# A hybrid decoder layer on one core: earlier fetches of kept results, finished rows on GpSimd's queue, and loads tied to products

## The chip, the cores and the metric

The kernel runs on one core of one Trainium2 chip. The metric is device time in microseconds (us), from the start to the end of one execution. A result is the median of several executions. The engines are named as in the profile: PE is TensorE's matmul pipe and PEld its weight loads, DVE is VectorE, ACT is ScalarE, POOL is GpSimd, SP is the engine that only issues DMAs here. A DMA that an engine issues goes through that engine's queue.

## The reference

One decoder layer over 2048 tokens of width 1024, in float32. Constants: 8 query heads and 2 key-value heads of 64, a window of 128, a causal convolution of 31 taps over 512 channels, and an inner width of 2816.

```python
hn = rms_norm(h, mix_pre_g)
proj = hn @ w_in                       # q, k, v and the input of the convolution
attn_out = sliding_window_attention(q, k, v, attn_sinks, rel_bias)
conv_out = conformer_conv(u, ...)      # GLU, 31 taps, layer norm, silu, pointwise product
mixed = concatenate([attn_out, conv_out]) @ w_out
h = h + rms_norm(mixed, mix_post_g)
hn = rms_norm(h, ffn_pre_g)
ff = (silu(hn @ w_gate) * (hn @ w_up)) @ w_down
h = h + rms_norm(ff, ffn_post_g)
```

## The kernel before, in words

**Products.** Each float32 operand is split into a high and a low part in fp32r (`split_w`, `split_f`, `lo`): ACT copies the high part, DVE or POOL subtracts it to get the low part. A product then takes three matmuls of 128x512 per block of 128 in the contraction, all of them recorded at line L85. Nearly all DVE operations are recorded at one line too, L94, so they are told apart by the names of their tiles. A letter behind the @ is the stage: A input projection, B attention, C convolution, W output projection, H operands of the channel mixer, F gate and up products, G down products.

**Stages.** The 2048 tokens are four tiles of 512 (0 to 3). A0 to A3 are the input projections, 14 units of 24 matmuls each; `load_x` (L253) loads the transposed x of a tile in four loads of 512 KB, `row_norms` (L267) loads x again in rows of 128 tokens for the norms, and `weight` and `kweight` load a unit's weights (L137) and store their low parts for the later tiles (L131). Attention B0 to B3, the taps of the convolution (`stage_taps`, DVE) and its tail run beside them. W0 to W3 are the output projection with its norm. They store the rows of h to `h_scr`, and the rows' transposes to `hT`.

**The channel mixer** runs twice: F0 and G0 for tokens of the tiles 0 and 1, F2 and G2 for 2 and 3. Gate and up are computed by a scheme of seven block products in place of eight, over sums of weight blocks and sums of operand blocks. Two of the seven products need no sums, and `stage_pre` does these ahead for the first pairs: in steps of 12 matmuls it goes twice over 20 (F0) or 16 (F2) blocks. In the first half a step's result is copied by ACT (`fa@F`) and stored to DRAM (`keeps`, L980). In the second half `fetch` (L943) loads the kept result into a buffer `gb`, `seed` (L959) copies it on ACT into a PSUM bank, and the step's matmuls are accumulated on top. Gate's result goes through silu on ACT. Up's is multiplied to it on DVE (`fa@F<-fa@F,mm@F`), and the product is stored to `mids` (L991). A step `q` splits the weights of step `q+3`, loads those of `q+4`, fetches the kept result of `q+2` and seeds `q+1`. Then `stage_p1` does the remaining products. It loads weight blocks (L1011, L1013, tiles `raw@F` and `chl@F`), and DVE forms their sums (`chl@F`), which are split (`w@F`).

**Beside them.** `stage_h_sums` (S0, S2) loads rows of `hT` (L888, `chl@H`) and forms the operand sums on DVE. `stage_tsums` (TS) forms differences of blocks of w_down for G0 and G2: its loads (L1126) and stores (L1138) go through POOL's queue, and its subtractions are tied to the matmul last emitted, which sets the order only and adds no wait on data. `finish` ends the rows of G0: a square, a gain, an inverse root, a load of the rows of h (L1155, `chl@G<-h_scr`), an addition on DVE (x@G, p@G) and two stores of the result (L1159).

**What sets the order.** The main line of stages is emitted step by step, and each step gives a time by which side lanes are pumped (`Lane`): one for attention, one for the taps, one for finished rows, one for operand sums, one for TS (rate RT = 0.2), and so on. A lane collects `dt * rate` as credit, at most 6.0, and emits while it has some. Priorities follow that order, and a scheduler in front of the engines sorts each engine's instructions by them, so that the program has one fixed order on each engine. Buffers are rings by tag: `chl` 5, `gb` 2, `at` 2, `raw` 2, `w` 6, `mm` (PSUM) 4. An engine runs its list in order, SP's and POOL's DMA issues included: an issue that waits for its data holds those behind it.

Of the kernel before, what the change touches and what calls it, by code (L numbers as in the profile page):

```python
# [25 lines left out]
P = 128  # L26
T = 512
# [10 lines left out]
def layer_kernel(ctx, tc, x, xT, cols, rows, sinks, relb, onehot, w_in, w_pw, w_out, w_gate, w_up, w_down, out):  # L38
# [135 lines left out]
    def after_first(first, r, how="NoSync"):  # L174
# [4 lines left out]
            reason="products of half the array stand together",  # L179
        )  # L180

    def three(o, pairs, first=True, last=True):
        n = 3 * len(pairs)
        i = 0
        for (sh, sl), (mh, ml) in pairs:
            for a, b in ((sh, mh), (sh, ml), (sl, mh)):
                mat(o, a, b, start=first and i == 0, stop=last and i == n - 1)
                i += 1
# [59 lines left out]
    def load_x(t):  # L248
        lab[0] = f"A{t}"
        xs = []  # L250
        for i in range(4):
            xt = f4("x", (P, 2, T))
            nc.sync.dma_start(xt, xT[2 * i : 2 * i + 2, :, t * T : (t + 1) * T].rearrange("c p t -> p c t"))  # L253
            xs.append(xt)
        started.add(f"x{t}")
        return [xs]
# [3 lines left out]
    def row_norms(ts, tag):  # L260
        lab[0] = f"A{ts[0]}"
        n = 4 * len(ts)
        ssq = sm(n)
        for i in range(n):
            xt = f4(tag)
            r0 = ts[0] * T + i * P
            nc.sync.dma_start(xt, x[r0 : r0 + P])  # L267
            act(junk, xt, AF.Square, accum_out=ssq[:, i : i + 1])
        r = rsqrt(ssq, n, D)
        for j, t in enumerate(ts):  # L270
            rn[t] = r[:, 4 * j : 4 * j + 4]
# [405 lines left out]
    def stage_x():  # L677
        lab[0] = "X0"
        rel = cst.tile([32, 8], F32, name="rel")
        nc.sync.dma_start(rel, relb)  # L680
        oh = f2("fa", (P, 2 * P))
        nc.sync.dma_start(oh[0:32], onehot)
        pb = tr()
        mat(pb[0:8, 0 : 2 * P], rel, oh[0:32], start=True, stop=True)
        bs = f2("fa", (P, 2 * P))
        nc.vector.tensor_copy(bs[0:8], pb[0:8, 0 : 2 * P])
        b_scr = dr.tile([8, 2 * P], F32, name="b_scr")
        nc.sync.dma_start(b_scr, bs[0:8])
        yield 8
        lab[0] = "X0"  # L690
        flip = f2("fa", (P, P))
        nc.gpsimd.memset(flip, 0.0)
        nc.gpsimd.affine_select(
            out=flip, in_=flip, compare_op=ALU.not_equal, fill=1.0, base=1 - P, pattern=[[1, P]], channel_multiplier=1
        )
        up = t_("mb", (P, 8, P))
        nc.sync.dma_start(up, bass.AP(tensor=b_scr.tensor, offset=b_scr.offset, ap=[[1, P], [2 * P, 8], [1, P]]))
        yield 8
        lab[0] = "X0"
        t = t_("mb", (P, 8, P))  # L700
        for n in range(2):
            o = tr()
            mat(o, flip, up[:, 4 * n : 4 * n + 4].rearrange("p h k -> p (h k)"), start=True, stop=True)
            nc.vector.tensor_copy(t[:, 4 * n : 4 * n + 4].rearrange("p h k -> p (h k)"), o)
        bias.append(t)
        yield 0.1
# [214 lines left out]
    def stage_pre(ws, ops, mid, keep, q0=0, q1=None):  # L921
# [17 lines left out]
        def fetch(q):  # L939
            if PRE <= q < q1:  # L940
                lab[0] = L
                kept[q] = f2("gb")
                nc.sync.dma_start(kept[q], keep[q - PRE])  # L943

        def split(q):
# [19 lines left out]
        for q in range(q0, q1):  # L965
            half, m = divmod(q, PRE)
            started.add(f"P{ws[0]}.{q}")
            bn = "B21" if half else "B11"
            if len(ops.get(bn, ())) < 4:
                lh.until(f"{bn}.{ws[0]}")  # L970
            split(q + 3)
            load(q + 4)
            fetch(q + 2)
            lab[0] = L
            seed(q + 1)
            lab[0] = L
            o = seeded.pop(q) if half else mm()
            product(o, wops.pop(q), ops[bn], not half)
            while pend:
                nc.sync.dma_start(*pend.pop())  # L980
            if not half:
                u = f2("fa")
                act(u, o, AF.Copy)
                pend.append((keep[m], u))
            else:
                if MATS[m][0] is w_gate:
                    sg = f2("fa")
                    act(sg, o, AF.Silu)
# [130 lines left out]
    def stage_tsums(td):  # L1119
        L = "G0"  # L1120
        for pr in range(NF // 2):
            lab[0] = L
            wx = f4("wx", (P, 2, T))
            b = [wx[:, 0], wx[:, 1], f2("fc"), f2("fc")]
            for i, (f, n) in enumerate(((0, 0), (0, 1), (1, 0), (1, 1))):
                nc.gpsimd.dma_start(b[i], w_down[2 * pr + f, :, n * T : (n + 1) * T])  # L1126
            yield 3.9
            b11, b12, b21, b22 = b
            for to, o, p_, q_ in ((0, b11, b12, b11), (2, b12, b22, b12), (1, b22, b22, b11), (3, b21, b21, b22)):
                lab[0] = L  # L1130
                r = vtt(o, p_, q_, ALU.subtract)
                tc.add_manual_dep(
                    r.ins,
                    made["rows"][-1].name,
                    mybir.DependencyInfo(mybir.DependencyClass.NoSync, mybir.DependencyReason.DATA),
                    reason="weight differences keep pace with the products",
                )
                nc.gpsimd.dma_start(td[to, pr], o)  # L1138
                yield 0.25

    def finish(L, gb, jobs, pool=True):
        lab[0] = L
        n_ = len(jobs)
        ssq = sm(4)
        for j, (rows_, halves) in enumerate(jobs):
# [6 lines left out]
        r = rsqrt(ssq[:, 0:n_], n_, 1, pool)  # L1152
        for j, (rows_, halves) in enumerate(jobs):
            ht = f4("chl" if L == "G0" else "mid")
            nc.sync.dma_start(ht, h_scr[rows_])  # L1155
            for n in range(2):
                cs = slice(n * T, (n + 1) * T)
                stt(halves[n], halves[n], r[:, j : j + 1], ht[:, cs], ALU.mult, ALU.add)
                nc.sync.dma_start(out[rows_, cs], halves[n])  # L1159
            yield 2.0  # L1160
            lab[0] = L

# [157 lines left out]
    class Lane:  # L1320
        def __init__(self, rate, lag):
# [4 lines left out]
            self.credit = 0.0  # L1326
            self.done = {}
            self.hold = lambda: False

        def add(self, name, gen, needs=None):  # L1330
            self.items.append((name, gen, needs))

        def pump(self, dt):
            if self.hold():
                return
            self.credit = min(self.credit + dt * self.rate, 6.0)
            while self.items and self.credit > 0:
                name, gen, needs = self.items[0]
                self.rate = self.rates.get(name, self.rate)
# [54 lines left out]
    lh.rates = {"N1": 1.2, "S0": 0.8, "B21.2": 0.5, "S2": 0.8}  # L1394
    lf.rates = {n: 0.6 for n in ("O0.1", "O0.3", "E0.1", "E0.3")} | {n: 1.2 for n in ("Y0", "Y1", "O2.1", "O2.3")}
    lc.rates = {"T0": RC0, "T1": RC1, "T2": RC2, "T3": RP}
    lw.rates = {"W0": RW0, "C2": RW, "W2": RW, "C3": RW, "W3": RW}

    def run(gen):
# [67 lines left out]
    del normed[:]  # L1467
    lh.add("S0", stage_h_sums(ws, ops), lambda: "N1" in lh.done)
    run(stage_pre(ws, ops, mids[0], keeps[0], Q0))
    lt.add("TS", stage_tsums(td))  # L1470
    run(stage_p1(ws, ops, mids[0], keeps[0]))
    lt.until("TS")
# [80 lines left out]
```

## Time and profile before

| | before |
|---|---|
| median of 3 runs | 1951.76 us (1948.69 to 1952.41) |
| profiled execution | 1951.41 us |
| its span, first to last instruction | 1949.7 us |
| mean granted TensorE clock | 0.993 |
| matmuls in the trace | 8730 |

The profile is of one execution. Its span leaves out 1.7 us of the execution's own time. Three views of it are used. The table of waits lists, for each engine, what ended its idle time: the engine and line waited for, us in total, times, the longest. The stretches list, for a piece of the span, each engine's busy time with the count of its instructions, the granted clock (PEclk), the mean busy share of the core's 16 DMA engines and what they moved. The timeline lists instructions by their start, with the idle time before them and what ended it in brackets; equal ones in a row are put together, and x24 is their count.

### The profile page before, as it was taken

To read this page: it belongs to the slowest core of one execution; us is meant where nothing else is said; L and a number is where in the kernel's file an instruction comes from. 1 tells how busy PE (TensorE), PEld (TensorE's weight loads), DVE (VectorE), ACT (ScalarE), POOL (GpSimd) and SP (SyncE) were. 2 spreads that over 40 slices of the span, in tenths; PEclk is the share of its full clock that TensorE was granted. 3 is DMA by queue.
4 is the path that set the end of the run, shared out by engine and by line. 5 is a ranking of instruction groups with operands and counts; after the bars stand their busy time and mean duration, and the time that the engine had idled before them with its cause. 6 is when DMAs were issued, how large, how long until landed. Compare 5 with 4: busy or idle time off the path is not lost.

```text
span 1949.7 us, 26646 instructions
## 1 busy us (share of the span) xinstructions
PE 1902.9 (98%) x8730; PEld 1537.4 (79%) x8730; DVE 1475.9 (76%) x2648; ACT 958.6 (49%) x1886; POOL 299.0 (15%) x427
## 2 busy tenths in 40 slices
PE   8999999999999999999999999998999999999997
PEld 6777777777777787788888788886788888888886
DVE  4999979995986998888579945578677776465557
ACT  5355455457658433334353555476534333345453
POOL 4011021011120111120000100000032333211003
PEclk9999999999999999999999999998999999999998
DMA  8787667667758767676477876769645443375663
GB/s 308 250 309 229 220 209 236 199 206 237 245 199 288 269 227 257 241 269 228 144 272 240 315 249 206 237 235 362 216 159 162 154 154 103 124 252 185 206 199 141
DMA packets 209578, 435.67 MB, mean 223 GB/s; under 512 B 21752, under 2 KB 39328, under 8 KB 209440
## 3 DMA queue, kind: packets, MB, share of 16 engines
q1 hardware_dynamic: 191648, 402.52, 61.8%
q0 software_dynamic: 7040, 23.07, 3.4%
q10 hardware_dynamic: 10752, 8.39, 1.3%
q8 instruction: 68, 1.11, 0.2%
q14 instruction: 70, 0.57, 0.1%
HBM read 323.26 MB, written 110.63 MB: 223 GB/s over the span
## 4 chain that ended last, share of the span: by engine, by line
PE 67%; DVE 15%; DMA 10%; issue 4%; ACT 2%; POOL 2%; SPq 1%; DVEq 0%; POOLq 0%; ACTq 0%
PE mm@F L85 30%; PE mm@G L85 17%; PE mm@A L85 8%; DVE fc@C L94 5%; PE mm@W L85 4%; PE tr@W L85 3%; PE tr@B L85 2%; DMA mids<-fa@F 2%; DVE w@F L94 1%; DMA keeps<-fa@F 1%; DVE chl@F L94 1%; DVE fa@F L94 1%; DMA w@W<-fold 1%; DMA gb@F<-keeps 1%; PE tr@B L504 1%
## 5 line engine op out<-in xcount | busy, mean ns | idle before, releaser
L94 DVE SCALAR_TENSOR_TENSOR fc@C<-glu@C,colt,fc@C 128x512 f32<-128x512 f32 x480 | 359.0, 762 | 2.7
L85 PE MATMUL mm@F<-hl@H,w@F 128*128 128x512 f32 x1056 | 261.1, 398 | 14.8 <-ACT mm@F L959 13.6
L85 PEld LDWEIGHTS mm@F<-hl@H,w@F 128*128 128x128 f32 x1056 | 201.1, 192 | 61.6 <-ACT mm@F L959 17.7
L85 PE MATMUL mm@G<-hl@G,hl@G 128*128 128x512 f32 x924 | 227.4, 393 | 1.8 <-DVE hl@G L94 1.8
L841 ACT ACTIVATE w@F<-chl@F 128x512 fp32r<-128x512 f32 x220 | 136.3, 626 | 186.3 <-PE mm@F L85 164.8
L85 PE MATMUL mm@A<-hl@A,w@A 128*128 128x512 f32 x840 | 207.9, 395 | 4.0 <-ACT w@A L127 2.1
L85 PEld LDWEIGHTS mm@G<-hl@G,hl@G 128*128 128x128 f32 x924 | 171.6, 188 | 38.3 <-DVE hl@G L94 2.6
L85 PE MATMUL mm@G<-w@G,hl@G 128*128 128x512 f32 x876 | 199.4, 389 | 0.0
L94 DVE TENSOR_TENSOR w@F<-chl@F,w@F 128x512 fp32r<-128x512 f32 x198 | 151.0, 765 | 59.9 <-ACT w@F L841 59.7
L85 PEld LDWEIGHTS mm@G<-w@G,hl@G 128*128 128x128 f32 x876 | 164.5, 188 | 34.1
L85 PEld LDWEIGHTS mm@A<-hl@A,w@A 128*128 128x128 f32 x840 | 155.2, 188 | 43.2 <-issue 3.9
L85 PE MATMUL mm@F<-mid@H,w@F 128*128 128x512 f32 x528 | 132.7, 392 | 0.8 <-DVE fa@F L94 0.8
L85 PE MATMUL mm@F<-ql@H,w@F 128*128 128x512 f32 x528 | 130.1, 391 | 0.7 <-ACT w@F L841 0.7
L85 PE MATMUL mm@F<-p@H,w@F 128*128 128x512 f32 x528 | 129.1, 389 | 0.0
L85 PE MATMUL mm@F<-x@H,w@F 128*128 128x512 f32 x528 | 125.7, 391 | 0.0
L85 PEld LDWEIGHTS mm@F<-mid@H,w@F 128*128 128x128 f32 x528 | 99.8, 189 | 22.3 <-ACT at@F L1086 1.2
L85 PEld LDWEIGHTS mm@F<-x@H,w@F 128*128 128x128 f32 x528 | 98.7, 188 | 21.3 <-issue 0.8
L85 PEld LDWEIGHTS mm@F<-p@H,w@F 128*128 128x128 f32 x528 | 99.1, 188 | 20.6
L85 PEld LDWEIGHTS mm@F<-ql@H,w@F 128*128 128x128 f32 x528 | 98.5, 188 | 21.1 <-ACT w@F L841 1.1
L507 POOL TENSOR_SCALAR_AFFINE_SELECT p@B<-p@B 128x512 f32<-128x512 f32 x62 | 56.6, 918 | 338.1 <-ACT p@B L505 336.6
L127 ACT ACTIVATE w@A<-raw@A 128x512 fp32r<-128x512 f32 x110 | 67.4, 626 | 82.4 <-PE mm@A L85 50.3
L94 DVE TENSOR_TENSOR w@G<-raw@G,w@G 128x512 fp32r<-128x512 f32 x73 | 53.6, 734 | 71.7 <-ACT w@G L841 70.7
(316 smaller groups left out, 3240.0 us busy)
## 6 DMA issues: line engine op xcount, KB each, us to landing
mids<-fa@F SPq DMA_DIRECT2D x154, 256.0 KB, 3.0
raw@A<-w_in SPq DMA_DIRECT2D x55, 512.0 KB, 4.5
w@A<-lo_in SPq DMA_DIRECT2D x84, 256.0 KB, 3.8
fc@G<-mids SPq DMA_DIRECT2D x77, 256.0 KB, 3.4
fa@G<-mids SPq DMA_DIRECT2D x75, 256.0 KB, 4.5
gb@F<-keeps SPq DMA_DIRECT2D x72, 256.0 KB, 4.0
w@W<-fold SPq DMA_DIRECT2D x32, 512.0 KB, 5.7
chl@F<-w_gate SPq DMA_DIRECT2D x22, 512.0 KB, 4.8
```

Of the source, the lines that this page charges most:

```text
L85: r = nc.tensor.matmul(*args, **kw)
L94: r = op(*args, **kw)
L127: act(w[:, 0], raw, AF.Copy)
L504: nc.tensor.transpose(o[:, i * P : (i + 1) * P], pr[:, 4 * g + i], ident)
L507: cut = nc.gpsimd.affine_select(out=pg[:, kb].rearrange("p (i q) -> p i q", q=P), in_=pg[:, 1].rearrange("p (i q) -> p i q", q=P), compare ...
L841: act(w[:, 0], x, AF.Copy)
```

## The change

Six edits, none of which changes what is computed:

1. A helper `tied` sets an instruction's order behind the matmul last emitted. The loads of `load_x` and `row_norms` are tied so; the differences of `stage_tsums` were already.
2. `stage_x`, which prepares the relative bias, yields 6 ahead of its first matmul, and 12 instead of 8 at its end.
3. `stage_pre` fetches a kept result four steps ahead instead of two, and the results go by turns into the buffers `gb` and `at`.
4. `finish` issues G0's loads of `h_scr` and its stores to `out` from POOL instead of SP: 8 loads of 512 KB and 16 stores of 256 KB. G2's stay on SP.
5. The lane of the taps collects 0.6 of its credit from the point where A3 has started and the convolution's tail of tile 0 is done, until W0 is done.
6. The lane of TS starts with a credit of 0 in place of what it had saved up.

```diff
+    def tied(r):
+        tc.add_manual_dep(
+            r.ins,
+            made["rows"][-1].name,
+            mybir.DependencyInfo(mybir.DependencyClass.NoSync, mybir.DependencyReason.DATA),
+            reason="keeps pace with the products",
+        )
+        return r
@@ load_x
-            nc.sync.dma_start(xt, xT[2 * i : 2 * i + 2, :, t * T : (t + 1) * T].rearrange("c p t -> p c t"))
+            tied(nc.sync.dma_start(xt, xT[2 * i : 2 * i + 2, :, t * T : (t + 1) * T].rearrange("c p t -> p c t")))
@@ row_norms
-            nc.sync.dma_start(xt, x[r0 : r0 + P])
+            tied(nc.sync.dma_start(xt, x[r0 : r0 + P]))
@@ stage_x
+        yield 6
+        lab[0] = "X0"
         pb = tr()
...
-        yield 8
+        yield 12
@@ stage_pre
-                kept[q] = f2("gb")
+                kept[q] = f2(("gb", "at")[q % 2])
                 nc.sync.dma_start(kept[q], keep[q - PRE])
...
-            fetch(q + 2)
+            fetch(q + 4)
@@ stage_tsums
-                r = vtt(o, p_, q_, ALU.subtract)
-                tc.add_manual_dep(
...
+                tied(vtt(o, p_, q_, ALU.subtract))
@@ finish
+        queue = nc.gpsimd if L == "G0" else nc.sync
...
-            nc.sync.dma_start(ht, h_scr[rows_])
+            queue.dma_start(ht, h_scr[rows_])
...
-                nc.sync.dma_start(out[rows_, cs], halves[n])
+                queue.dma_start(out[rows_, cs], halves[n])
@@ Lane
+            self.share = lambda: 1.0
...
-            self.credit = min(self.credit + dt * self.rate, 6.0)
+            self.credit = min(self.credit + dt * self.rate * self.share(), 6.0)
@@ the program
+    lc.share = lambda: 0.6 if "A3" in started and "C0" in ld.done and "W0" not in lw.done else 1.0
...
+    lt.credit = 0.0
     lt.add("TS", stage_tsums(td))
```

The order of the instructions moves at three places. The rows below give line, operation, output and inputs with the tiles' numbers, and shape.

SP at the start of the program, before, with some stores of low parts (`lo_in`) and one load for the fold left out; `raw@A` are weight tiles of the first units, `x@A` and `p@A` the two kinds of loads of x:

```order
L137 DMA raw@A_32_271<-w_in 128x1024
L253 DMA x@A_43_334<-xT 128x2x512
L680 DMA rel<-relb 32x8
L267 DMA p@A_63_448<-x 128x1024
L253 DMA x@A_44_336<-xT 128x2x512
L267 DMA p@A_64_451<-x 128x1024
L267 DMA p@A_65_454<-x 128x1024
L267 DMA p@A_66_457<-x 128x1024
L253 DMA x@A_45_338<-xT 128x2x512
L131 DMA lo_in<-w@A_24_213 128x512
L253 DMA x@A_46_340<-xT 128x2x512
L137 DMA raw@A_47_342<-w_in 128x1024
```

The same place of the change:

```order
L137 DMA raw@A_32_271<-w_in 128x1024
L689 DMA rel<-relb 32x8
L131 DMA lo_in<-w@A_24_213 128x512
L131 DMA lo_in<-w@A_25_217 128x512
L137 DMA raw@A_47_342<-w_in 128x1024
L137 DMA raw@A_53_390<-w_in 128x1024
L262 DMA x@A_43_334<-xT 128x2x512
L262 DMA x@A_44_336<-xT 128x2x512
L262 DMA x@A_45_338<-xT 128x2x512
L262 DMA x@A_46_340<-xT 128x2x512
L137 DMA raw@A_68_471<-w_in 128x1024
```

The third weight tile, `raw@A_47`, stood behind four loads of `x@A` and four of `p@A`; now none of the eight stands ahead of it. The four of `x@A` follow two weight tiles later, and the four of `p@A` further on, ahead of the seventh.

SP at the end of F2's `stage_pre`, before; `fa@F` is a finished product on its way to `mids`, `chl@F` the first weight block of `stage_p1`:

```order
L936 DMA raw@F_2168_12973<-w_gate 128x512
L936 DMA raw@F_2168_12973<-w_up 128x512
L943 DMA gb@F_2153_12886<-keeps_4719 128x512
L943 DMA gb@F_2157_12907<-keeps_4719 128x512
L1013 DMA chl@F_2184_13086<-w_gate 128x1024
L1182 DMA fc@G_2555_15619<-mids_4716 128x512
L991 DMA mids_4716<-fa@F_2155_12902 128x512
L943 DMA gb@F_2161_12931<-keeps_4719 128x512
L943 DMA gb@F_2165_12952<-keeps_4719 128x512
```

The same place of the change, a little later in the list:

```order
L1002 DMA mids_4703<-fa@F_2173_12996 128x512
L1022 DMA raw@F_2183_13084<-w_gate 128x1024
L1054 DMA gb@F_2201_13150<-keeps_4706 128x512
L1022 DMA raw@F_2190_13103<-w_up 128x1024
L1002 DMA mids_4703<-fa@F_2179_13036 128x512
L899 DMA chl@H_2135_12796<-hT_116 128x2x512
L1054 DMA gb@F_2219_13254<-keeps_4706 128x512
L1002 DMA mids_4703<-fa@F_2182_13068 128x512
L1024 DMA chl@F_2184_13086<-w_gate 128x1024
L1024 DMA chl@F_2191_13105<-w_up 128x1024
```

The load of `chl@F_2184` stood ahead of the stores of the last five products (its list goes on with them); now it stands behind the store of the last one, `fa@F_2182`, and the last load of S2, `chl@H_2135`, has come down to just ahead of that store.

DVE at the start of F0's `stage_p1`, before; `at@F` is an accumulated block product, `wx@G` and `fc@G` are the blocks of w_down in TS, `fc@C` a tap:

```order
L94 TENSOR_TENSOR wx@G_1119_6658<-wx@G_1119_6658 128x512
L94 SCALAR_TENSOR_TENSOR fc@C_1083_6465<-glu@C_1082_6463,colt,fc@C_1083_6465 128x512
L94 TENSOR_TENSOR at@F_1115_6639<-at@F_1115_6639,mm@F_1113_6624 128x512
L94 TENSOR_TENSOR at@F_1123_6680<-at@F_1123_6680,mm@F_1114_6626 128x512
L94 TENSOR_TENSOR w@F_1140_6777<-chl@F_1108_6613,w@F_1140_6777 128x512
L94 TENSOR_TENSOR w@F_1147_6814<-chl@F_1143_6796,w@F_1147_6814 128x512
```

The same place of the change:

```order
L94 TENSOR_SCALAR fc@C_1125_6664<-glu@C_1124_6662,colt 128x512
L94 SCALAR_TENSOR_TENSOR fc@C_1125_6664<-glu@C_1124_6662,colt,fc@C_1125_6664 128x512
L94 TENSOR_TENSOR at@F_1113_6622<-at@F_1113_6622,mm@F_1111_6607 128x512
L94 SCALAR_TENSOR_TENSOR fc@C_1125_6664<-glu@C_1124_6662,colt,fc@C_1125_6664 128x512
L94 TENSOR_TENSOR at@F_1118_6647<-at@F_1118_6647,mm@F_1112_6609 128x512
L94 TENSOR_TENSOR w@F_1137_6748<-chl@F_1106_6596,w@F_1137_6748 128x512
L94 TENSOR_TENSOR w@F_1144_6779<-chl@F_1140_6767,w@F_1144_6779 128x512
```

Ahead of the first two `at@F` stood a difference of TS, the fifth of the kernel; now no difference stands there, and the first one comes eight rows further on.

More of the change, by code (lines that the diff above doesn't have):

```diff
@@ L1130, in stage_tsums @@
                 lab[0] = L
-                r = vtt(o, p_, q_, ALU.subtract)
-                tc.add_manual_dep(
[L1133 to L1137, printed above, removed]
+                tied(vtt(o, p_, q_, ALU.subtract))
                 nc.gpsimd.dma_start(td[to, pr], o)
```

## The prediction

> **What bounds the kernel now.** I read the page's head first, then TensorE's waits over the whole span, then the stretches in which those waits lie.
>
> ```profile
> span 1949.7 us, 26646 instructions
> PE 1902.9 (98%) x8730; PEld 1537.4 (79%) x8730; DVE 1475.9 (76%) x2648; ACT 958.6 (49%) x1886; POOL 299.0 (15%) x427
> ```
> TensorE is busy 1902.9 of 1949.7 us, so all its idle time is 46.8 us. The change leaves out no matmul. It can win only idle time, and the time that matmuls take longer after an idle stretch. The table of TensorE's waits says who ended that idle time (total us, times, longest):
>
> ```profile
> PE mm@F L85 <- ACT mm@F L959: 13.6, 7, 5.1
> PE mm@F L85 <- DVE at@F L94: 3.7, 2, 2.3
> PE mm@W L85 <- DVE x@W L94: 2.1, 1, 2.1
> PE mm@A L85 <- ACT w@A L127: 2.1, 2, 1.9
> ...
> PE tr@B L85 <- DVE sm@A L94: 1.1, 1, 1.1
> ...
> PE mm@A L85 <- POOL w@A L129: 0.6, 1, 0.6
> ```
> One cause stands out: L959, `seed`, which copies a kept result into a PSUM bank before the second half of `stage_pre` adds to it. TensorE's timeline in F2 shows five of those waits one behind the other:
>
> ```profile
> 1341.07 7.57 PE L85 MATMUL mm@F<-hl@H,w@F 128*128 128x512 f32 x24 [2.65 <-ACT mm@F L959]
> 1353.74 8.43 PE L85 MATMUL mm@F<-hl@H,w@F 128*128 128x512 f32 x24 [5.10 <-ACT mm@F L959]
> 1363.38 3.04 PE L85 MATMUL mm@F<-hl@H,w@F 128*128 128x512 f32 x12 [1.21 <-ACT mm@F L959]
> 1367.55 3.04 PE L85 MATMUL mm@F<-hl@H,w@F 128*128 128x512 f32 x12 [1.13 <-ACT mm@F L959]
> 1372.55 7.79 PE L85 MATMUL mm@F<-hl@H,w@F 128*128 128x512 f32 x26 [1.96 <-ACT mm@F L959]
> ```
> They add up to 12.05 us. The waits are not the whole loss, which the stretches of 40 us show (us, then each engine's busy time and count, the granted clock, the DMA share, GB/s):
>
> ```profile
> 640.00:680.00 40.00, 36.92 (x155) 29.63 (x154) 36.63 (x60) 19.07 (x35) 5.92 (x11) 0.96 0.82 272
> 672.00:676.00 4.00, 3.29 (x9) 2.62 (x10) 3.44 (x7) 3.24 (x6) 0.68 (x2) 0.68 0.79 240
> 1320.00:1360.00 40.00, 32.24 (x126) 25.20 (x125) 34.88 (x82) 25.32 (x53) 0.00 (x0) 0.87 1.02 370
> 1360.00:1400.00 40.00, 35.70 (x148) 28.37 (x147) 27.52 (x42) 21.95 (x40) 1.52 (x1) 0.96 0.76 260
> 1400.00:1440.00 40.00, 40.00 (x178) 33.12 (x177) 26.59 (x32) 15.01 (x28) 11.08 (x7) 1.00 0.46 147
> ```
> The undisturbed stretch of 1400 to 1440 holds 178 matmuls, 0.2247 us each. The two ahead of it hold 126 and 148, so 52 + 30 = 82 matmuls are missing: 82 x 0.2247 = **18.4 us**. 12.05 of that is waiting. The other 6.4 fits the granted clock of 0.87 and 0.96, which lacks 0.17 x 40 = 6.8 us of full speed. This is what can be won in F2.
>
> **F2: the fetches.** Why the seed is late can be read from SP's queue, where one fetch stands among stores and loads, and from the landings between 1280 and 1376:
>
> ```profile
> 1346.41 0.33 SPq L943 DMA_DIRECT2D gb@F<-keeps  x1
> ```
> ```profile
> chl@G<-h_scr SPq DMA_DIRECT2D x8, 512.0 KB, 6.4
> ...
> gb@F<-keeps SPq DMA_DIRECT2D x12, 256.0 KB, 5.5
> ...
> out<-p@G SPq DMA_DIRECT2D x8, 256.0 KB, 5.1
> ...
> chl@F<-w_gate SPq DMA_DIRECT2D x1, 512.0 KB, 3.7
> ```
> The fetch issued at 1346.41 feeds the step that starts at 1353.74, after 5.10 us of waiting. A step is 12 matmuls, 2.7 us; two steps are 5.4 us, against a median of 5.5 us from issue to landing, and SP's other entries come before the issue. So two steps ahead is not enough. Four steps ahead is 10.8 us, and in the new order the fetches stand some 30 matmuls (6.7 us) or more before their use. The finished rows' 24 DMAs leave SP's queue as well. I take all five waits and the slow clock as gone: **-18.4 us**.
>
> **F2: what is late next.** The same edits let the finished rows and S2's operand sums slip behind the products: the loads `chl@H<-hT` stand at matmul 6094, 6144, 6194 and 6242 now, against 6059, 6086, 6110 and 6134 before. Their sums stand among VectorE's products and weight splits, at this pitch:
>
> ```profile
> 1363.42 0.68 DVE L94 TENSOR_TENSOR w@F<-raw@F,w@F 128x512 fp32r<-128x512 f32 x1
> 1364.02 0.68 DVE L94 TENSOR_TENSOR chl@H<-mid@G,chl@H 128x512 f32<-128x512 f32 x1
> ```
> That is 0.60 us from start to start. Two places follow.
> - Step 28 needs the low half of a weight split. From the product of step 25 on, VectorE has that product, ten operand sums, the product of step 27 and the split in its queue: 13 x 0.60 = 7.8 us. TensorE does two steps meanwhile, 5.4 us. The difference is a wait of **+2.4 us**.
> - The first load of `stage_p1`, `chl@F<-w_gate`, now stands behind the last store of `mids`, which waits for the last product of `stage_pre`. Counted from the end of the last matmul: the product 0.8 us, two issues on SP 0.7, landing 3.7 (the row above), then five VectorE operations up to the first split, 3.0, and the latencies between: about **+8.4 us** without a matmul. Before, this load stood some 96 matmuls (22 us) ahead. This price has two ends: 0, if the products run late enough for the loads to be far ahead, and some 10 us with the landing of 5.5.
> - After such a gap the clock is lower for a while. The stretch of 672 to 676 above shows 0.68 behind one wait of 2.29 us. I take one such time, 3.4 us at half speed: **+1.7 us**.
>
> F2 thus wins 18.4 - 2.4 - 8.4 - 1.7 = **5.9 us**. The gap of 8.4 us is what I am least sure of, and the row 1320 to 1360 sets another limit: the DMA engines are full there (1.02, 370 GB/s), and moving a fetch forward moves no byte out of that stretch; the rows that slip do.
>
> The Trainium skill, "TensorE: Matmul & The Clock Gate", section "What's actually happening", has the clock halve after an idle window of about 3.4 us that runs freely. The fall after 2.29 us in the row of 672 does not agree with that as a minimum for a single wait. By the page alone the wait at step 28 costs no clock, by the row it may cost another 1.7 us; the sum goes by one slow time.
>
> **The start.** TensorE waits at 32.44 and 33.80 for the third weight tile, whose load stands on SP behind eight loads of x:
>
> ```profile
> 32.44 0.73 PE L85 MATMUL mm@A<-hl@A,w@A 128*128 128x512 f32 x2 [1.93 <-ACT w@A L127]
> 33.80 2.57 PE L85 MATMUL mm@A<-hl@A,w@A 128*128 128x512 f32 x10 [0.62 <-POOL w@A L129]
> ```
> ```profile
> 11.89 0.38 SPq L253 DMA_DIRECT2D x@A<-xT  x1
> 21.63 0.33 SPq L137 DMA_DIRECT2D raw@A<-w_in  x1
> ```
> From 11.89 to 21.63 those eight loads, 512 KB each, go ahead of the weight tile. Tied to matmuls, they stand behind it: -1.93 - 0.62 = -2.55 us. They then stand ahead of later weight tiles: 4 x 512 KB of x before one and 4 x 512 KB before another. At the 370 GB/s of the row above, 2 MB take 5.7 us, so a new wait of 0 to 4 us can come near 52 us. I take 0.55 and book **-2.0 us**. The wait of 1.1 us for `sm@A` at 119 us goes too, since the loads of x that held VectorE's work there come later: **-1.1 us**.
>
> **F0.** Of L959's 13.6 us, 13.6 - 12.05 = 1.5 us lie in F0, and the earlier fetch takes them away. The other wait there is VectorE's:
>
> ```profile
> 670.70 0.69 DVE L94 TENSOR_TENSOR wx@G<-wx@G 128x512 f32<-128x512 f32 x1 [1.72 <-DMA wx@G<-w_down]
> ```
> ```profile
> 672.71 2.36 PE L85 MATMUL mm@F<-yt@H,w@F 128*128 128x512 f32 x6 [2.29 <-DVE at@F L94]
> ```
> A difference of `stage_tsums` waited 1.72 us for its data, and the accumulation `at@F` that TensorE needed stood behind it. With the credit at nothing, the first differences come some 28 VectorE rows later, so they hold nothing back there: -2.29 us, and -1.7 for the slow clock of the row 672 to 676. F0: -1.5 - 2.29 - 1.7 = **-5.5 us**. The second wait for `at@F` (3.7 - 2.3 = 1.4 us) stays.
>
> **W0 and G0.** The wait for `x@W` (2.1 us at 384) is that of the first output projection, at which the share of 0.6 is aimed. Around that place the new order has as many taps as the old one, 78 against 74 in 500 matmuls, and the heap of VectorE work ahead of it stays: **0**, with -2.1 and +1 as ends. In G0 the taps of T3 end some 100 matmuls later; the tight places move and do not go: **+0.5**, between -0.3 and +1.5. The extra yield in `stage_x` and 24 issues on GpSimd instead of SP add no work on TensorE: 0. For small waits at new places that I have not found: **+1.5**.
>
> Of the rows on GpSimd's queue the trace shows only transfers of another kind, those of `stage_tsums`:
>
> ```profile
> 661.20 0.54 POOL L1138 DMA_DIRECT2D td<-wx@G  x1 [2.52 <-DVE wx@G L94]
> ```
> ```profile
> fc@G<-w_down POOLq DMA_DIRECT2D x22, 256.0 KB, 5.2
> ```
> An issue takes 0.54 us against 0.33 on SP, and the landing, 5.2 us, is that of SP's `out<-p@G` (5.1). In 1320 to 1360 POOL is idle (0.00), so nothing stands ahead of those rows; I price the move at nothing. The Trainium skill, "DMA: Bandwidth & Descriptors", section "SWDGE vs HWDGE vs iDMA", speaks against it: DMAs from GpSimd get their descriptors by software, in memory that VectorE can lock it out of. No row here shows such a delay: the landing agrees with SP's, while VectorE is busy 36.63 of 40 us around that issue (row 640 to 680).
>
> **The sum.** -5.9 - 2.0 - 1.1 - 5.5 + 0.5 + 1.5 = -12.5 us against the profiled execution's own 1951.41 us gives 1938.9. The median of the runs, 1951.76, lies 0.35 above that execution, so the median forecast is **1939**.
>
> **The rivals.**
> - *F2 gives nothing back.* VectorE's sums and the load for `stage_p1` are early enough in time though late in the order. For it: the load has no data to wait for, only a queue. Against it: SP issues in order, and the store ahead of it waits for the last product. The 12.5 us of new waits in F2 go: 1926.5.
> - *F2 gives all of it back.* The DMA share of 1.02 speaks for it: with the queue full, the tied loads and fetches land later, and S2's sums meet VectorE's products. Another 5.9 us: 1945.
> - *No change.* F2 gives all back, the loads of x take 4 us at 52 us instead of 0.55, and F0's differences hold another accumulation. About 1951.
> - *Slower, by GpSimd's queue.* Four groups of finished rows each load `h_scr`, and VectorE's additions stand in order ahead of products and splits. If a load takes 13 us there instead of 6.4, each group holds VectorE for 6.6 us, 26.4 in all, of which VectorE's idle time in 1320 to 1360 (40 - 34.88 = 5.1 us) covers a part: 1939 + 21 = 1960. It turns the sign from a landing of some 11 us on. Against it stands the landing of 5.2.
>
> **How the numbers follow.** A measurement of this kernel can tell a difference of about 0.2%, 3.9 us, from none. The forecast, 1939 with 1932 to 1944 of its own, gets 0.45; nothing given back 0.17; all given back 0.23; no change 0.08; slower 0.07. The first three are faster by more than 3.9 us: 0.85. The range reaches to them, 1924 to 1948, and leaves out 0.15.
>
> **What would show it.** In the profile after: no waits for L959 in F2, and the fetches landing before the bank is free; a gap of 8 us at the first matmul of F2's `stage_p1`, ended by the split of `chl@F`, and one of 2 to 3 us some 48 matmuls earlier; no wait at 32 us, perhaps one near 52 us; no wait for `at@F` at 672; 2.1 us still at 384. The prediction is wrong if waits for L959 stay in F2, if the gap ahead of `stage_p1` is under 3 or over 12 us, or if the rows on GpSimd's queue land in more than 11 us.

## The result and the profile after

The changed kernel is slower by half a per cent: 1960.68 us (median of 4 runs, 1959.42 to 1962.01) against 1950.70 for the kernel before (median of 4, the three runs given above and one more), a ratio of 1.0052 with a 95% interval of 1.0034 to 1.0069. The same kernel on another chip, beside later experiments, gave 1.0034 (1.0020 to 1.0048). The profiled execution took 1959.68 us, its span 1958.0. The line of the engines' busy time on its page:

```profile
PE 1907.0 (97%) x8730; PEld 1541.7 (79%) x8730; DVE 1481.9 (76%) x2648; ACT 960.8 (49%) x1886; POOL 315.8 (16%) x451
```

TensorE has 51.0 us of idle time in place of 46.8, and its matmuls took 4.1 us longer. The number of matmuls is the same in both traces, so the k-th matmul of one can be set against the k-th of the other. Worked out from the start times of the matmul records (a few transposes change places, which blurs a single row by 1 or 2 us):

| matmul number | before, us | after, us | difference | change since the row above | place |
|---|---|---|---|---|---|
| 200 | 51.3 | 49.8 | -1.5 | -1.5 | first units of A0 |
| 300 | 76.1 | 84.3 | +8.2 | +9.7 | A0 |
| 800 | 174.9 | 182.3 | +7.5 | -0.7 | A1 |
| 1000 | 215.8 | 230.9 | +15.0 | +7.5 | A2 |
| 3000 | 616.4 | 631.3 | +14.8 | -0.2 | A2 to F0's `stage_pre`, W0 among it |
| 4200 | 900.1 | 905.2 | +5.1 | -9.7 | F0 |
| 6000 | 1302.4 | 1309.6 | +7.2 | +2.0 | G0, W3 |
| 6300 | 1386.5 | 1382.5 | -4.0 | -11.2 | F2's `stage_pre` |
| 6400 | 1409.2 | 1417.1 | +7.9 | +11.9 | F2's `stage_p1` begins |
| 8700 | 1930.5 | 1938.4 | +7.9 | 0.0 | the rest |

So F0 did win, and F2 won and gave it all back. The loss was made at the start and in A2. TensorE's waits over the span, after (total us, times, longest):

```profile
PE mm@F L85 <- ACT w@F L852: 7.9, 2, 7.2
PE mm@A L85 <- ACT w@A L127: 5.6, 3, 5.1
PE mm@F L85 <- ACT mm@F L970: 5.2, 7, 1.2
PE mm@A L85 <- DVE ql@A L94: 4.8, 1, 4.8
PE tr@B L85 <- DVE sm@B L474: 3.1, 1, 3.1
...
PE mm@F L85 <- DVE at@F L94: 0.4, 1, 0.4
```

The seed's wait (line L970 now) has fallen from 13.6 to 5.2 us, and the one for `at@F` from 3.7 to 0.4. New are the waits for the weights of F2's `stage_p1` (`w@F`), the weights of A0 (`w@A`), `ql@A`, and attention's `sm@B` (at 399 us, beside W0).

**The start.** TensorE's and SP's timeline after:

```profile
59.99 1.22 PE L85 MATMUL mm@A<-hl@A,w@A 128*128 128x512 f32 x2 [5.07 <-ACT w@A L127]
61.55 1.22 PE L85 MATMUL mm@A<-hl@A,w@A 128*128 128x512 f32 x2 [0.34 <-ACT w@A L127]
64.18 2.07 PE L85 MATMUL mm@A<-hl@A,w@A 128*128 128x512 f32 x4 [1.41 <-DVE w@A L94]
```
```profile
29.14 2.01 SPq L262 DMA_DIRECT2D x@A<-xT  x4
32.20 0.68 SPq L137 DMA_DIRECT2D raw@A<-w_in  x1
34.65 0.33 SPq L137 DMA_DIRECT2D raw@A<-w_in  x1
45.04 1.86 SPq L276 DMA_DIRECT2D p@A<-x  x4
51.62 1.63 SPq L137 DMA_DIRECT2D raw@A<-w_in  x2
```

The waits at 32 and 34 us are gone. But between 34.65 and 51.62 SP issues no weight load. For the first half of that time, up to 43.41, it issues nothing at all: its next entry is a store of a low part (`lo_in`), and GpSimd can make that low part only from the weight tile whose load, issued at 32.20 behind the four `x@A`, took 9.08 us. The chain of work shows the load and GpSimd's operation, and SP's waits from 30 to 53 us the store (L131):

```profile
32.20 9.08 DMA raw@A<-w_in
...
42.10 1.28 POOL w@A L129
```
```profile
SPq L131 <- POOL w@A L129: 7.8, 2, 7.5
```

Only then come the four `p@A`, and the next weight load stands behind them. When it is issued, they are still landing. ScalarE's copy of that tile says when the load came:

```profile
59.31 1.15 ACT L127 ACTIVATE w@A<-raw@A 128x512 fp32r<-128x512 f32 x2 [3.08 <-DMA raw@A<-w_in]
```

From issue to use 7.7 us pass, and TensorE waits 5.07. The clock falls with it; the stretches of 4 us after (busy times by engine, granted clock, DMA share, GB/s):

```profile
60.00:64.00 4.00, 2.44 (x4) 0.99 (x4) 2.26 (x7) 2.01 (x4) 1.72 (x9) 0.50 0.57 183
64.00:68.00 4.00, 3.82 (x9) 3.05 (x10) 4.00 (x8) 0.00 (x0) 0.00 (x0) 0.50 0.77 203
1400.00:1404.00 4.00, 2.87 (x7) 1.84 (x6) 4.00 (x7) 2.31 (x4) 0.43 (x1) 0.50 0.78 251
```

For 8 us the clock is at 0.50, which is how 6.8 us of waits (5.07 + 0.34 + 1.41) become 9.7 us of loss.

**A2.** TensorE waits 4.81 us for an operand that VectorE makes, after a stretch in which VectorE is busy without a break:

```profile
191.18 4.96 PE L85 MATMUL mm@A<-mid@A,w@A 128*128 128x512 f32 x12 [4.81 <-DVE ql@A L94]
```
```profile
170.00:180.00 10.00, 10.00 (x52) 8.10 (x52) 9.93 (x24) 7.86 (x26) 1.90 (x2) 1.00 0.43 150
180.00:190.00 10.00, 6.37 (x35) 3.88 (x35) 10.00 (x17) 5.87 (x11) 0.00 (x0) 0.93 0.56 163
```

The third busy time is VectorE's: 9.93 and 10.00 of 10 us, and it is 9.79 to 9.96 in the 20 us before. In the kernel before VectorE is as full there (9.71 to 10.00 in each 10 us from 150 to 190), but TensorE, the first busy time, does not wait:

```profile
170.00:180.00 10.00, 10.00 (x56) 7.87 (x53) 10.00 (x20) 6.44 (x13) 0.00 (x0) 1.00 0.51 163
180.00:190.00 10.00, 10.00 (x55) 8.07 (x54) 9.71 (x29) 5.85 (x14) 1.50 (x2) 1.00 0.96 336
```

What differs is the order within the full stretch. The granted clock is 0.50 from 191 to 195 us, which makes 7.5 us of the 4.81.

**F2.** TensorE's waits for the seed from 1300 to 1420, after, and the end of its timeline there:

```profile
PE mm@F L85 <- ACT mm@F L970: 4.9, 6, 1.2
```
```profile
1380.24 0.73 PE L85 MATMUL mm@F<-hl@H,w@F 128*128 128x512 f32 x2 [0.64 <-ACT w@F L852]
1381.45 10.72 PE L85 MATMUL mm@F<-hl@H,w@F 128*128 128x512 f32 x46 [0.48 <-DVE w@F L94]
1399.40 1.22 PE L85 MATMUL mm@F<-mid@H,w@F 128*128 128x512 f32 x2 [7.23 <-ACT w@F L852]
1401.75 4.64 PE L85 MATMUL mm@F<-mid@H,w@F 128*128 128x512 f32 x10 [1.13 <-DVE w@F L94]
```

The five long waits for the seed became six short ones, 4.9 us in place of 12.05. Ahead of `stage_p1` stands the gap, 7.23 + 1.13 = 8.36 us. The chain of work through it names the load behind the last store and what VectorE still had to do:

```profile
1392.54 0.61 DVE fa@F L94
1393.16 0.32 SPq L1002
...
1393.53 4.45 DMA chl@F<-w_gate
...
1398.60 0.68 DVE chl@F L94
1399.29 0.60 DVE x@H L94
...
1401.09 0.61 DVE w@F L94
```

**GpSimd's queue.** The landings of the finished rows after, between 1280 and 1376:

```profile
chl@G<-h_scr POOLq DMA_DIRECT2D x8, 512.0 KB, 7.7
...
out<-p@G POOLq DMA_DIRECT2D x8, 256.0 KB, 6.0
```

7.7 us in place of 6.4, and 6.0 in place of 5.1. The larger effect is on SP's own fetches beside them. Their landings, for those issued from 1340 to 1366 us, before and after:

```profile
DMA to landing us min/median/max: 5.7/6.6/6.8
```
```profile
DMA to landing us min/median/max: 7.7/9.6/13.5
```

A seed that TensorE waits for starts when such a fetch lands:

```profile
1357.39 0.60 ACT L970 ACTIVATE mm@F<-gb@F 128x512 f32<-128x512 f32 x1 [2.36 <-DMA gb@F<-keeps]
```

The fetch goes out two steps earlier than in the kernel before, 5.4 us by the prediction's step of 2.7; the longer landings take 3.0 us of that back at the median, and at the longest more than all of it (6.7).

### The profile page after: what moved, and what is told of

It reads as the page before. It is cut to its first block, busy times and chain, and to the rows that moved or that the text cites. A ratio compares the mean times of both kernels' runs of the same rounds, so it can differ in the third digit from the quotient of the medians.

```text
span 1958.0 us, 26660 instructions
## 1 busy us (share of the span) xinstructions
PE 1907.0 (97%) x8730; PEld 1541.7 (79%) x8730; DVE 1481.9 (76%) x2648; ACT 960.8 (49%) x1886; POOL 315.8 (16%) x451
## 4 chain that ended last, share of the span: by engine, by line
PE 79%; DVE 8%; DMA 7%; issue 2%; ACT 2%; POOL 1%; SPq 1%; DVEq 0%; POOLq 0%; ACTq 0%
PE mm@F L85 37%; PE mm@G L85 18%; PE mm@A L85 10%; PE tr@W L85 4%; PE mm@W L85 3%; DVE fc@C L94 3%; PE tr@B L85 2%; PE mm@U L85 1%; PE tr@B L513 1%; DMA raw@F<-w_up 1%; DMA w@A<-lo_in 1%; DMA fa@G<-mids 1%; DMA mids<-fa@F 1%; DMA raw@F<-w_gate 1%; DMA raw@A<-w_in 1%
## 5 line engine op out<-in xcount | busy, mean ns | idle before, releaser
L85 PE MATMUL mm@F<-hl@H,w@F 128*128 128x512 f32 x1056 | 254.8, 391 | 6.4 <-ACT mm@F L970 5.2
```

Source lines behind the costliest of these rows:

```text
L85: r = nc.tensor.matmul(*args, **kw)
```

## The experiments

Each kernel was timed against the kernel before on the same chip; the ratios are to that, with 95% intervals. The unaltered change stands at 1.0052 and 1.0034. Beside the ratio the profile gives the length of a stretch between two matmul numbers, which shows where a difference lies:

| | 0 to 300 | 800 to 1000 | 3000 to 4200 (F0) | 4200 to 6000 (G0) | 6000 to 6400 (F2) |
|---|---|---|---|---|---|
| before | 74.5 | 41.0 | 283.7 | 402.3 | 106.8 |
| the change | 82.6 | 48.5 | 274.0 | 404.3 | 107.5 |
| c_after (the change again) | 82.0 | 48.4 | 276.7 | 404.2 | 108.2 |
| u_loads | 72.4 | 42.0 | 274.7 | 403.6 | 109.1 |
| u_rows | 70.9 | 47.5 | 275.3 | 402.5 | 107.3 |
| u_x | 71.0 | 47.4 | 275.5 | 408.6 | 108.7 |
| t1_tied | 80.8 | 44.4 | 273.4 | 403.7 | 106.3 |
| t23_tied | 73.0 | 47.5 | 278.7 | 402.6 | 108.1 |
| u_credit | 79.6 | 48.6 | 283.0 | 403.0 | 105.5 |
| u_fetch | 81.4 | 49.1 | 278.6 | 404.6 | 107.7 |
| u_share | 83.2 | 48.6 | 275.2 | 406.7 | 94.4 |
| u_finish | 79.3 | 50.0 | 277.3 | 402.9 | 99.4 |
| f_loads_sp | 80.4 | 49.4 | 275.5 | 403.8 | 103.4 |
| f_stores_sp | 81.5 | 48.0 | 275.1 | 402.5 | 104.9 |
| w_wx | 74.2 | 41.8 | 275.4 | 404.6 | 105.2 |
| b_fin_wx | 73.7 | 40.6 | 275.2 | 404.2 | 98.3 |
| b_fin_wx_share | 74.1 | 40.6 | 275.1 | 405.4 | 92.6 |

Kernels whose edits do not touch a stretch still differ there by 4 us, in G0 by 6 (the first column from 79.3 to 83.2 where the first loads are tied; F2 from 105.5 to 109.1 where its edits are as in the change; G0 from 402.5 to 408.6). A difference below that is not read as one. The same kernel run twice, the change and c_after, differs by 0.1 to 2.7 us.

### The tied loads

**u_loads**: both kinds of loads free again.

```diff
-            tied(nc.sync.dma_start(xt, xT[...]))
+            nc.sync.dma_start(xt, xT[...])
-            tied(nc.sync.dma_start(xt, x[r0 : r0 + P]))
+            nc.sync.dma_start(xt, x[r0 : r0 + P])
```

> The changed kernel with the loads of load_x and row_norms no longer tied; all else as changed. Theory (the ties cost the start and A2): the row loads no longer stand just ahead of the weight tile that TensorE waits 5.07 us for at 60 us, and x of tile 2 comes some 130 matmuls earlier, so the wait of 4.81 at 191 us goes; some 10 and 6 us with the slow clock; the wait of 2.5 us at 32 us comes back. 1960.7 - 10 - 6 + 2.5 = 1947, faster than before. Rival (the ties are harmless, the taps' share and the lanes make these waits): within 3 us of 1960.7, with a wait of 4 to 5 us left at 191.

1946.73 us, 0.9954 (0.9940 to 0.9967): faster than before. The start is 10 us shorter than in the change, A2 6.5, and the wait for `ql@A` is 1.1 us. The ties made the loss; the rest of the change is a gain.

**u_rows**: the second of these two edits alone.

> The changed kernel with only the row loads (row_norms) untied; load_x stays tied. Theory that the four row loads are what the weight tile at 60 us stands behind, and that x of tile 2 makes the wait at 191: the wait at 60 goes (about -10), a wait near 32 us comes back (1 to 2.5), the one at 191 stays: about 1953. Rival that the four loads of x (at matmul 97) fill the queue as well: half of the wait at 60 stays, 1957.

0.9995 (0.9981 to 1.0010). The wait at 60 us is gone and the start is at 70.9, shorter even than in u_loads; no wait over 0.3 us stands at 32. `ql@A` stays, with 6.4 us.

**u_x**: the first alone.

> The changed kernel with only load_x untied; the row loads stay tied. By the theory the wait of 5 us at 60 stays (the row loads stand at matmul 170 as in the changed kernel) and the one of 4.8 at 191 goes: 1960.7 - 6 = 1955. Rival that the row loads of tiles 2 and 3 make the wait at 191: it stays, and the total is within 3 us of 1960.7.

1.0014 (1.0004 to 1.0023). Here the theory failed in its first half: the wait at 60 is gone as well, though the row loads stand where they stood. SP's timeline of this kernel shows why:

```profile
38.21 0.39 SPq L137 DMA_DIRECT2D raw@A<-w_in  x1
42.37 0.45 SPq L137 DMA_DIRECT2D raw@A<-w_in  x1
44.35 2.03 SPq L276 DMA_DIRECT2D p@A<-x  x4
```

With the `x@A` gone ahead of the first weight tiles, two more weight tiles are issued before the four `p@A`. It is not one group that blocks. With both groups tied, the four `x@A` and the four `p@A` stand among the weight loads within 18 us (29.14 to 46.9), and no weight tile is issued in the 17 us that follow 34.65; with either group elsewhere, the weight loads keep their pace. SP's longest wait for GpSimd's `w@A` from 30 to 53 us says the same: 7.5 us in the change, 6.6 in c_after and 8.2 in t1_tied below, which all have the wait at 60, but 0.8 in u_rows and 1.9 in u_x. `ql@A` stays here too, with 4.9 us, so the second half of the theory, that x of tile 2 alone makes it, is not enough either.

**c_after, t1_tied, t23_tied**: the change again, and the ties of tile 1 or of tiles 2 and 3 alone.

```diff
-            tied(nc.sync.dma_start(xt, xT[...]))
+            (tied if t == 1 else lambda r: r)(nc.sync.dma_start(xt, xT[...]))
-            tied(nc.sync.dma_start(xt, x[r0 : r0 + P]))
+            (tied if ts[0] == 1 else lambda r: r)(nc.sync.dma_start(xt, x[r0 : r0 + P]))
```

(`t > 1` and `ts[0] > 1` in t23_tied.)

> The changed kernel itself, unaltered, beside the next two on the same chip. Both theories expect its known ratio to before, 1.004 to 1.007. It shows how much the start and A2 differ from one execution to the next when nothing is changed: waits of 4 to 6 us at 60 us and at 191 us if both belong to the program.

> The changed kernel with ties only on the loads of tile 1; those of tiles 2 and 3 are free. Theory that the ties of tile 1 make the wait at 60 us and those of tiles 2 and 3 the wait at 191: the wait at 60 stays, the one of ql@A goes below 2 us, 5 to 6 us faster than c_after. Rival that the wait at 191 is the backlog left by the start, since VectorE is full from 150 to 200 us: both waits stay, total within 2 us of c_after.

> The mirror: ties only on the loads of tiles 2 and 3. By the theory the wait at 60 goes, some 9 us, and the one of ql@A stays at 4 to 6 us. By the rival both go, some 15 us faster than c_after, as u_loads.

c_after 1.0034 (1.0020 to 1.0048), with waits of 5.57 at 60 us and 5.16 for `ql@A`: both belong to the program. t1_tied 1.0008 (0.9995 to 1.0022), t23_tied 0.9994 (0.9979 to 1.0010). TensorE's timelines of these two, t1_tied first:

```profile
59.22 1.22 PE L85 MATMUL mm@A<-hl@A,w@A 128*128 128x512 f32 x2 [4.96 <-ACT w@A L127]
...
190.46 3.04 PE L85 MATMUL mm@A<-mid@A,w@A 128*128 128x512 f32 x12 [1.34 <-DVE ql@A L94]
```
```profile
180.76 5.49 PE L85 MATMUL mm@A<-mid@A,w@A 128*128 128x512 f32 x12 [3.50 <-DVE ql@A L94]
```

The wait at 60 belongs to tile 1's loads, and most of the one at 191 to the loads of tiles 2 and 3, not to a backlog that the start leaves. Tile 2's normalized operands need its x and its rows' norms, so either one late is enough, which is why u_rows and u_x both kept the wait. The traces agree: where either is tied (the change, c_after, u_rows, u_x, t23_tied), VectorE begins the last of the eight multiplications of tile 2's x when 802 to 812 matmuls have started, and TensorE waits 3.5 to 6.4 us for `ql@A` behind it; where both are free (the kernel before, u_loads, t1_tied, w_wx), when 790 to 800 have, and the wait is 1.3 us or less. VectorE has no free time there to make that up.

### The credit of TS

**u_credit**:

```diff
-    lt.credit = 0.0
```

> The changed kernel without the credit of TS set to nothing. F0 won 9.9 us in the changed kernel from matmul 3000 to 3900. Theory that the later differences of w_down are what freed VectorE there: the waits for at@F come back and 4 to 8 us of the 9.9 go, 1965 to 1969. Rival that the earlier fetch won it: F0 keeps its 9.9 us, 1960 to 1962.

1.0076 (1.0057 to 1.0094), a median of 1971.34 us; the profiled execution, 1963.91, is the fastest of its six. F0 takes 283.0 us in it, as in the kernel before; the 6 to 9 us that F0 won are gone. The waits for `at@F` are back, the longest of them at another place (829 us):

```profile
PE mm@F L85 <- ACT at@F L1094: 3.7, 2, 3.4
PE mm@F L85 <- DVE at@F L94: 2.1, 3, 1.3
```

### F2

**u_fetch**: the fetches two steps ahead, in `gb` alone.

```diff
-                kept[q] = f2(("gb", "at")[q % 2])
+                kept[q] = f2("gb")
-            fetch(q + 4)
+            fetch(q + 2)
```

> The changed kernel with the fetch of kept results as before: two steps ahead, buffers gb alone. In the built order this also brings the first load of stage_p1 from matmul 6254 to 6206 and its sums ahead of the last product. Theory (the fetch won the waits for seed and cost the gap ahead of stage_p1): the gap of 7.2 + 1.1 us goes with its slow clock, some -11; the waits for seed come back to 10 to 13 us with their slow clock, some +11; the total within 3 us of the changed kernel (ratio to before 1.004 to 1.007). Rival (the DMA engines are full, and the fetch distance matters little): the waits for seed stay near 5 us, and the total falls by 8 us or more (1.001 or less).

1.0041 (1.0025 to 1.0057). In F2 the two are equal, 107.7 against 107.5 and 108.2, and made up as the theory has it. A row of TensorE's waits in this kernel:

```profile
PE mm@F L85 <- ACT mm@F L970: 14.0, 7, 4.1
```

The seed's waits are back, and the gap is gone: `w@F` on ScalarE, 7.9 us in the change, is 0.7 here. In F0 the stretch is 2 to 5 us longer, little more than the spread there.

**u_share**:

```diff
-    lc.share = lambda: 0.6 if "A3" in started and "C0" in ld.done and "W0" not in lw.done else 1.0
+    lc.share = lambda: 1.0
```

> The changed kernel with the taps' credit not cut (share 1.0). In the built order S2's loads stand 30 to 40 matmuls earlier and the first load of stage_p1 at 6242 instead of 6254. Theory (fewer taps early push T3, W3, the finished rows and S2 later, and so make a part of the gap ahead of stage_p1): the gap shrinks from 8.4 to about 5 us, F2 wins 3 to 5; at W0 the waits grow by 0 to 2; total ratio to before 1.002 to 1.005. Rival (the cut of the taps does what it is aimed at): waits of 3 us or more appear around W0 and the total does not fall.

0.9983 (0.9969 to 0.9996). F2 is 13 us shorter, more than expected. Ahead of `stage_p1` the gap of 8.36 us is all but gone, 0.43, since the first sums of `chl@F` are done before the last product; the 3.14 us in the first row is the earlier wait for a weight split, 1.12 in the change:

```profile
1383.34 12.80 PE L85 MATMUL mm@F<-hl@H,w@F 128*128 128x512 f32 x48 [3.14 <-ACT w@F L852]
...
1397.59 2.58 PE L85 MATMUL mm@F<-mid@H,w@F 128*128 128x512 f32 x10 [0.43 <-DVE w@F L94]
```

The seed's waits have gone too, from 5.2 to 1.0 us. G0 is 2.4 us longer, within the spread. Around W0 the waits are 3.9 us for `sm@B` and 1.1 for `x@W`, against 3.1 and 0.7 in the change, so no new wait of 3 us appears. Without the cut S2's loads are issued 32 to 45 matmuls earlier than in the change; with it they come later, and it is F2 that pays.

**u_finish, f_loads_sp, f_stores_sp**: both, or one, of the finished rows' DMAs on SP again.

```diff
-        queue = nc.gpsimd if L == "G0" else nc.sync
+        queue = nc.sync
```

(In f_loads_sp only the load of `h_scr` is issued by SP, in f_stores_sp only the stores.)

> The changed kernel with G0's finished rows on SP again. Theory (the queue that issues them is indifferent; the DMA engines are full either way): the waits for seed stay 4 to 7 us and the gap ahead of stage_p1 7 to 9; total within 2 us of the changed kernel (1.004 to 1.007). Rival (SP's queue was the limit, or GpSimd's queue delays the rows): the waits for seed grow to 8 us or more, or F2 gets faster by 3 us or more.

> The changed kernel with G0's loads of h_scr on SP again and its stores to out still on GpSimd. u_finish (both on SP) won 8 us between matmuls 6000 and 6400. Theory (the burst of five 512 KB loads on a second queue stretches SP's raw@F load beside it, 11.57 us from issue to landing in the changed kernel, and SP's later fetches wait behind): all or most of the 8 us comes here, ratio to before 0.999 to 1.002. Rival (the sixteen stores on the second queue take the transfers' share): none of it, 1.004 to 1.006.

> The mirror of it: the changed kernel with G0's stores on SP and its loads of h_scr still on GpSimd. By the theory nothing is won in F2 (within 2 us of the changed kernel there, waits for seed 4 to 7 us); by the rival the 8 us come here and the waits for seed fall below 2 us.

u_finish 0.9988 (0.9975 to 1.0001): the theory that the queue is indifferent fell. F2 is 8 us shorter, and the waits for the seed are nearly gone:

```profile
PE mm@F L85 <- ACT mm@F L970: 1.3, 2, 0.8
```

The fetches issued from 1340 to 1366 us land fast again:

```profile
DMA to landing us min/median/max: 5.2/5.6/6.1
```

f_loads_sp 1.0016 (1.0003 to 1.0028) and f_stores_sp 1.0017 (1.0004 to 1.0031): F2 is 103.4 and 104.9, about 4 and 3 of the 8 us, and the longest landing of a fetch in that window is 10.0 and 11.6 us. Neither expectation held alone. Neither half gives the whole, since both intervals lie above that of u_finish; so it is not the burst of loads by itself. That the stores and the loads each give a part fits these numbers, but 104.9 is within 1 us of the spread, and so this is not shown for the smaller part. How the two queues share the DMA engines, no run here shows.

**w_wx**: u_loads with one buffer changed.

```diff
-                r1 = t_("chl", (P, 2, T))
+                r1 = t_("wx" if ws[0] and not m else "chl", (P, 2, T))
```

> u_loads (both kinds of loads untied) with the second half of F2's first stage_p1 weight block in the buffer wx, which is free there: in the built order its load comes some 2000 matmuls earlier, and nothing else of F2's loads moves. It tells which of two things makes the gap of 7.5 + 1.1 us ahead of stage_p1. If only the load behind the last store: the gap goes but for 1 us, 8 to 10 us faster than u_loads (ratio to before about 0.991). If VectorE's rest of S2 stands behind it (seven operations of 0.60 from the last product to the first split): a gap of 4.5 to 5.5 stays, 3 to 4 us faster than u_loads (0.9935 to 0.9945). If only VectorE: no change (0.995).

1941.6 us, 0.9924 (0.9905 to 0.9944). The gap after it:

```profile
1386.24 0.73 PE L85 MATMUL mm@F<-mid@H,w@F 128*128 128x512 f32 x2 [3.48 <-ACT w@F L852]
1388.59 3.42 PE L85 MATMUL mm@F<-mid@H,w@F 128*128 128x512 f32 x8 [1.62 <-DVE w@F L94]
```

5.10 us stay of 8.6. The late load made some 3.5 us of the gap. The larger part is VectorE's work behind the last product of S2: in this trace eight operations follow the product of 1383.04 without a break, up to and with the first split at 1387.85. Four of them are S2's and four `stage_p1`'s own.

### Versions that beat both

**b_fin_wx** is w_wx with the edit of u_finish, **b_fin_wx_share** that with the edit of u_share.

> w_wx (loads untied, the first block of stage_p1 in wx) with the finished rows on SP; the fetches four ahead, the credit of 0 and the taps' share stay. If the gains add up (13 us of u_loads and 4 of the buffer wx, seen in profiles, and 8 of u_finish): 1960.7 - 25 = 1936, ratio to before 0.988. If the DMA engines limit F2 whatever issues: 0.992, as w_wx.

> b_fin_wx with the taps' credit not cut. u_share lost 6 us up to matmul 6000 and won 13 in F2. If what it won in F2 is the same collision that u_finish takes away and the same gap that wx takes away: F2 wins at most 4 us more and the rest loses 6, ratio 0.989 to 0.991, slower than b_fin_wx. If it is of its own (S2 earlier, the sums ahead of the last product): F2 wins 7 or more beyond b_fin_wx, 0.986 to 0.988.

b_fin_wx: 1937.43 us, 0.9911 (0.9889 to 0.9932). b_fin_wx_share: 1937.44, 0.9909 (0.9888 to 0.9931). Both beat the kernel before and the change, and each other not at all. Against w_wx, 0.9924, the totals do not tell b_fin_wx apart; its F2 is 6.9 us shorter. In b_fin_wx_share F2 is 5.7 us shorter still, between the two ends expected; between matmuls 1000 and 3000 it takes 405.5 us in place of 400.8, which would eat most of the gain, but other kernels range from 398.8 to 407.0 there. The wait for `x@W` at W0, at which the cut is aimed, is 2.1 us with it and without it in these two. Of the six edits only the second, the yields of `stage_x`, was not tried alone.

## Why the prediction was wrong

It said 1939 us and faster; the kernel is slower. By the profile the sum is off by 20.4 us: +7.9 at matmul 8700 in place of -12.5. The start makes 10.2 of that, A2 7.5 and F2 6.6, while F0 won 4.2 more than forecast. By its own steps:

- **The start** (-2.0): the largest step that failed. "A new wait of 0 to 4 us can come near 52 us" had the cause right, and the size wrong. The waits come to 6.8 us and with the slow clock to 9.7, where 0.55 was taken. The working reckoned 2 MB as 5.7 us of one transfer. It left out that SP's queue is in order and is held twice: 7.5 us by the store of a low part, whose weight tile landed late behind the tied `x@A`, and then by the `p@A`, four stores and a load. The gain at 32 us came, with -1.5 at matmul 200 for the -2.55 of the step.
- **A2** (no term): missed, +7.5 us. The prediction moved the loads of tile 1 and booked -1.1 at 119 us for tile 2's later loads; that wait did go (matmuls 300 to 800: -0.7). That these loads feed VectorE in a stretch where it is full was in the profile before, in the stretches from 150 to 190 us.
- **F0** (-5.5): right in kind, larger in size, -9.7; u_credit puts 6 to 9 of it on the credit, as the step has it.
- **F2** (-5.9): +0.7. Up to matmul 6300 it won 11.2 us where the terms give 16.0 (18.4 less 2.4); behind that it lost 11.9 where they give 10.1. The gap was 8.36 us against 8.4 predicted, but in part by luck: the step made it of a landing of 3.7 us and five operations on VectorE, and w_wx shows that VectorE's work makes more of it than the load. Its slow clock cost 3.5 us (11.9 - 8.36) where 1.7 was taken from one slow time. The wait at step 28 was 1.12 against 2.4. What failed is "all five waits and the slow clock as gone": 4.9 us of waits for the seed stayed, which the prediction names as a sign of being wrong. The step costed the finished rows on GpSimd's queue at nothing, by their own landings in a stretch whose DMA share was 0.82, for a stretch where it was 1.02; SP's fetches beside them, reckoned at 5.5 us, took 7.7 to 13.5. u_finish puts the price of that at 8 us in F2. The Trainium skill, "DMA: Bandwidth & Descriptors", section "SWDGE vs HWDGE vs iDMA", has each DMA engine take turns between the queues of the two kinds; the result fits that, but no run here shows the turns.
- **W0** (0): -0.2 from matmul 1000 to 3000, as predicted, but by luck: the 2.1 us for `x@W`, which were to stay, fell to 0.7, and 3.1 for `sm@B` came. In u_loads, which keeps the cut of the taps, both are as before (2.1 and none), so both came with the ties. u_share shows the price of the cut elsewhere, 13 us in F2, which no term had.
- **G0** (+0.5) and small waits (+1.5): +2.0 in G0, the sum of the two, though the 1.5 was meant for the whole kernel.
- **The rivals.** "No change" comes nearest in mechanism: F2 gives all back, as it says, and the loads of x cost more than its 4 us; it does not have A2. "Slower" has the right sign, and its 1960 next to 1960.7 is a coincidence. It has GpSimd's queue delay the finished rows to a landing of 13 us; that landing was 7.7, under its threshold of 11. The queue did cost, but through SP's fetches: the seed's waits are 5.2 us with it and 1.3 without.

## What to carry to other kernels

A load that is moved later must be followed past everything behind it on its queue, the stores that wait for its neighbours' data included, and the lead that is used up twice in a short time counts once. A stage whose engine is full has no slack for later inputs, even when nothing waits there yet. Where the DMA engines are full, moving rows to another queue is no free change: look at the landings on the queue that they left, in the tight stretch, since a median over a longer one hides them. An edit that shifts work in one stage has to be priced where the displaced work lands.

## What the runs showed of the hardware

After the wait of 5.07 us the granted clock was 0.50 for 8 us (the rows from 60 to 68 above), and 0.50 in 1400 to 1404 behind the wait of 7.23; behind the wait of 2.29 us of the kernel before it was 0.68 over 4 us. Behind waits of 1.93 us (at 32 us) and 2.15 us (at 384) of the kernel before it stayed at 1.00 over the next 4 us. The same program's start, up to matmul 300, took 82.6 us in one execution and 82.0 in another, and F0 274.0 and 276.7, with nothing changed.
